# Attention heads with the low parts of the probabilities multiplied last, three outputs in another pool, and the second half of LN1 on ScalarE with a gate behind its transposes

## The chip, the cores and the metric

One Trainium2 chip, one core of it. The metric is the device time in microseconds of one execution; times stand as the median of several runs. A profile is one execution taken by the hardware profiler; its times count from the span's start.

## The reference, cut to what matters

One decoder layer over 512 tokens of width 1024, in float32. All weights are float32 too.

```python
h = layer_norm(x, ln_in_g, ln_in_b)
q_g, k_g, v_g, r_g, a_lr, q_lat, kv_lat, gate_logits = split(h @ w_in)
# branch 1: gated linear attention, 4 heads, chunked        -> y_gla
# branch 2: multi-head latent attention (MLA), 8 heads:
q = (rms_norm(q_lat) @ w_q_b)            # per head 128 "nope" + 64 "rope" columns
kv = (rms_norm(kv_lat[..., :256]) @ w_kv_b)   # per head 128 of k_nope + 128 of v
k_rope = apply_rope(kv_lat[..., 256:])   # shared by the heads
for blk in range(4):                     # 128 queries each, keys [0, block end)
    s = (q_nope @ k_nope.T + q_rope @ k_rope.T) * 192 ** -0.5
    p = softmax(where(causal, s, -inf))
    o[blk] = p @ v
y_mla = merge_heads(o) @ w_o_mla
mix = (g_gla * y_gla + g_mla * y_mla) @ w_out
h = layer_norm(2 ** 0.25 * h + mix, ln1_g, ln1_b)              # LN1
ff = square(relu(h @ w_ff1)) @ w_ff2                            # hidden width 4096
out = layer_norm(2 ** 0.25 * h + ff, ln2_g, ln2_b)
```

## The kernel before, in words

**Numbers in two parts.** A float32 operand is held as a high part (rounded to the matmul's float32r format) and a low part, the remainder. `split` (L111 and L112, with a scale L114 and L115) makes them: ACT writes the high part from PSUM, DVE then subtracts it from the source and writes the low part. A product takes three matmuls, high x high, high x low and low x high; low x low is left out. Weights stream from memory as `wraw` (or `wq`), and `pump` splits them into `whi` and `wlo` in the same way (L189 on ACT, L190 on DVE).

**Who fixes the order.** The program is traced once. Generators ("active") advance by one step at each `tick`, which the gemm helpers call between their steps; so parts of a head, of LN1 or of window sums are traced between matmuls. The tile framework then plans: it runs through the traced instructions with its own model of their times (`schedule_with_timeline_sim=True`), earlier traced ones first where several are ready, gives each tile a slot of its pool, and so fixes one order for each engine. On the chip each engine follows its list in order and waits by semaphores. `tc.issue_after(x)` binds an instruction to come after x on that engine's list.

**PSUM pools.** Eight banks: `pm` has four ("mm" tiles, `MM()`), `px` four ("px" tiles, `PX()`). The gemms of the projections, the feed-forward and the second column of the output take mm tiles; scores, transposes and head outputs take px tiles.

**The MLA heads.** `mla_pair(pr)` projects the queries (`gemm_fm`, 18 matmuls of 512 columns, two accumulators in mm) and keys (12) of heads 2pr and 2pr + 1, starts their generators `mla_head`, and projects their values (`gemm_tm`, 24 matmuls of 256 columns, two mm banks for four tiles; split into `mv` tiles). `mla_head` has four blocks of 128 queries: scores in a px bank (L1051 to L1053 for block 0, L1057 to L1061 for the others: three products of the nope parts, `qn` and `kn`, then two of the rope parts, `QS` and `KK`), mask and maximum on DVE (L1063), exponential with its sum on ACT (L1064), the normalisation on DVE (L1065, L1066). The probabilities are transposed on TensorE (L1078) into three px banks, and split into PT0 (keys 0 to 127), PT1 (128 to 255, and 384 to 511) and PT2 (256 to 383). The output is 12 matmuls in one px bank, for each key tile j: v high x p high (L1097), v high x p low (L1098), v low x p high (L1099). It is split into `omT`. While one head's softmax runs, TensorE works on the projections of the next pair, on the next head's scores or on the projection of the finished heads.

**LN1.** `out` is computed in two halves of 256 tokens, and its `ev_res` (L1407) adds it to the residual rows `res`. `ln1(hf)` normalises tiles 2hf and 2hf + 1: statistics on DVE (L429 to L431), the power -0.5 on POOL (L432), and one pass over the row on DVE (L438). `ln_transpose` then turns the rows on TensorE, two transposes of 128x128 for each of eight k (L447), and makes `h` with gain and bias (L450 on ACT for the high part, L452 on ACT or L454 on DVE, and L455 on DVE for the low part). While `ln1(1)` is under way, the first four blocks of the feed-forward's first weight are multiplied for tokens 0 to 255: `gemm_fm(PL["f1", 0, 0], ..., toks=slice(0, 256))`, 96 matmuls of 256 columns (32 turns of three). For k = 0 to 5 the four accumulators take turns; the last 24 matmuls, k = 6 and 7, follow for one accumulator after another. `finish(t_ln)` stands behind it, then come tokens 256 to 511.

**The window sums.** `win_sums` (L1486) adds and subtracts blocks of the second feed-forward weight on DVE, 128x1024 each, ahead of `win_f2`. They are held behind `st["ev"]` where that exists; before the change it is set by `win_f2` alone, so in the first window nothing holds them.

The lines that `ln_rows` already has for ScalarE, used before the change by the first tile of the input norm alone:

```python
        if on_act:
            nmr = S([P, 1], F32, "nmr")
            stt(nmr, mv[:, 0:1], -1.0, mv[:, 1:2], op0=ALU.mult, op1=ALU.mult)
            act(dst, src, AF.Identity, scale=mv[:, 1:2], bias=nmr)
```

Of the kernel before, what the change touches and what calls it, by code (L numbers as in the profile page):

```python
# [16 lines left out]
ALU = mybir.AluOpType  # L17
AX = mybir.AxisListType

P = 128  # L20
T = 512
D = 1024
NT = T // P
# [29 lines left out]
def tile_hybrid_block(ctx: ExitStack, tc: tile.TileContext, I, out, dbg=None):  # L53
# [178 lines left out]
    def part(x, i, c):  # L232
        return x[i][:, c] if isinstance(x, tuple) else x[:, i, c]

    def gemm_fm(pl, xs, n, evac, width=None, toks=slice(0, T), accs=None, guard=None, late=False):
        na = n // P
        accs = accs or [MM() for _ in range(na)]
        nk = pl["nk"]
        tail = range(nk - 2, nk) if pl["per"] == 2 and nk % 2 == 0 and not late else range(nk - 1, nk)
        turns = [(k, a) for k in range(tail[0]) for a in range(na)] + [(k, a) for a in range(na) for k in tail]  # L240
        for n_, (k, a) in enumerate(turns):
            hi, lo = weights(pl, k)
            xh, xl = part(xs[k], 0, toks), part(xs[k], 1, toks)
            c = slice(a * P, (a + 1) * P)
            o = accs[a][:, toks]
            mm(o, hi[:, c], xh, start=k == 0, stop=False)  # L246
            mm(o, hi[:, c], xl, start=False, stop=False)  # L247
            mm(o, lo[:, c], xh, start=False, stop=k == nk - 1)  # L248
            if (n_ + 1) % na == 0 and n_ + 1 < len(turns):
                tick(width)  # L250
        if guard:
            guard()
        if evac is not None:
            for a in range(na):
                evac(a, accs[a])
                if a == na // 2 - 1:
                    pump(pl["idx"][-1] + 1)
        tick(width)
        return accs
# [166 lines left out]
    def ln_rows(src, dst, mv, on_act=False):  # L426
        bst = S([P, 2, 6], F32, "bst")
        for j in range(2):
            nc.vector.bn_stats(bst[:, j, :], src[:, j * T:(j + 1) * T])  # L429
        nc.vector.bn_aggr(mv, bst)  # L430
        vts(mv[:, 1:2], mv[:, 1:2], LN_EPS, None, op0=ALU.add)  # L431
        gtt(mv[:, 1:2], mv[:, 1:2], mhalf[:, 0:1], op=ALU.pow)  # L432
        if on_act:
            nmr = S([P, 1], F32, "nmr")
            stt(nmr, mv[:, 0:1], -1.0, mv[:, 1:2], op0=ALU.mult, op1=ALU.mult)
            act(dst, src, AF.Identity, scale=mv[:, 1:2], bias=nmr)
        else:
            vts(dst, src, mv[:, 0:1], mv[:, 1:2], op0=ALU.subtract, op1=ALU.mult)  # L438

    def ln_transpose(rows, g, b, outs, hf, alt=False, n="h0"):  # L440
        tk = slice(hf * 256, (hf + 1) * 256)
        for k in range(NK):
            if len(outs) <= k:
                outs.append(A([P, 2, T], F32R, n) if n == "h0" else (B([P, T], F32R, n), B([P, T], F32R, n)))
            p = MM() if alt and k in (4, 5) else PX()
            for i in range(2):
                nc.tensor.transpose(p[:, i * P:(i + 1) * P], rows[2 * hf + i][:, k * P:(k + 1) * P], ident)  # L447
            tmp = B([P, 256], F32, "lnt")
            hi, lo = part(outs[k], 0, tk), part(outs[k], 1, tk)
            ha = act(hi, p[:, :256], AF.Identity, scale=g[:, k:k + 1], bias=b[:, k:k + 1])  # L450
# [583 lines left out]
    def mla_head(h, hl, qn, kn, vt):  # L1034
# [5 lines left out]
        for i in range(NT):  # L1040
            n = P * (i + 1)
            c = slice(i * P, (i + 1) * P)
            p = PX()
            o = p[:, :n]
            Pm = P02[:, :P] if i == 0 else P02[:, P:] if i == 2 else B([P, T], F32, "Pm")
            Pm = Pm[:, :n]
            mx = S([P, 1], F32, "mx")
            sme = S([P, 1], F32, "sme")
            if i == 0:
                o2 = p[:, :2 * P].rearrange("p (w n) -> p w n", w=2)  # L1050
                mm(o2, qn[:, 0, c], kn[:, :, :n], start=True, stop=False, skip_group_check=True)  # L1051
                mm(o, qn[:, 1, c], kn[:, 0, :n], start=False, stop=False, skip_group_check=True)
                mm(o2, qs[:, c], KK[:, :, :n], start=False, stop=True, skip_group_check=True)  # L1053
                vtt(Pm, p[:, P:2 * P], hide[:, T - n:], op=ALU.add)
                first = Pm
            else:
                mm(o, qn[:, 0, c], kn[:, 0, :n], start=True, stop=False)  # L1057
                mm(o, qn[:, 0, c], kn[:, 1, :n], start=False, stop=False)
                mm(o, qn[:, 1, c], kn[:, 0, :n], start=False, stop=False)
                mm(o, qs[:, c], KK[:, 0, :n], start=False, stop=False)  # L1060
                mm(o, qs[:, c], KK[:, 1, :n], start=False, stop=True)  # L1061
                first = hide[:, T - n:]
            nc.vector.tensor_tensor_reduce(Pm, o, first, -1.0, 3e38, op0=ALU.add, op1=ALU.min, accum_out=mx)  # L1063
            act(Pm, Pm, AF.Exp, bias=mx, scale=-1.0, accum_out=sme)  # L1064
            nc.vector.reciprocal(sme, sme)  # L1065
            vts(Pm, Pm, sme, None, op0=ALU.mult)  # L1066
            Ps.append(Pm)
            if i != 0:
                yield
# [12 lines left out]
        PT0, PT1, PT2 = PT  # L1082
        while vt[NT - 1] is None:
            yield
        o = PX()
        for j in range(NT):
            c = slice(hl * P, (hl + 1) * P)
            vh, vl = vt[j][:, 0, c], vt[j][:, 1, c]
            if j == 0:
                ph, pl, od = PT0[:, 0, :], PT0[:, 1, :], o  # L1090
            elif j == 1:
                ph, pl, od = PT1[:, 0, :384], PT1[:, 1, :384], o[:, 128:]
            elif j == 2:
                ph, pl, od = PT2[:, 0, :], PT2[:, 1, :], o[:, 256:]
            else:
                ph, pl, od = PT1[:, 0, 384:], PT1[:, 1, 384:], o[:, 384:]
            mm(od, vh, ph, start=j == 0, stop=False)  # L1097
            mm(od, vh, pl, start=False, stop=False)  # L1098
            mm(od, vl, ph, start=False, stop=j == NT - 1)  # L1099
        yield  # L1100
        om = A([P, 2, T], F32R, "omT")
        st["om"] = split(o, om[:, 0, :], om[:, 1, :])
# [316 lines left out]
    def ln1(hf):  # L1419
        for tt in (2 * hf, 2 * hf + 1):  # L1420
            mv = S([P, 2], F32, "mv")
            ln_rows(res[tt], res[tt], mv)
        yield
        for k, _ in enumerate(ln_transpose(res, ln1g, ln1b, h1T, hf, n="h1")):
            if k % 2:
                yield
# [5 lines left out]
    finish(t_ln)  # L1432
    st["gates"] = st["ln"]
    t_ln = spawn(ln1(1))
    accs = gemm_fm(PL["f1", 0, 0], h1T, T, None, toks=slice(0, 256))
    finish(t_ln)

    def residual1():
# [283 lines left out]
```

## Time and profile before

| | |
|---|---|
| median of 3 runs | 871.4 us (871.12 to 872.61) |
| profiled execution | 870.4 us, its span 868.6 us |
| TensorE busy | 849.6 us, 98% of the span, 4709 matmuls |
| VectorE busy | 635.7 us, 73% |
| ScalarE busy | 470.8 us, 54% |
| GpSimd busy | 146.2 us, 17% |
| mean granted TensorE clock | 0.997 |

In the profile's rows, a line of the timeline has the start, the duration, the engine, the kernel's line, the operation, the tile written and the tiles read, partitions x elements, and how many were merged; in brackets the idle time of that engine before it and what ended it. Matmuls overlap: the next starts before the one before has ended, so the pace is read from start to start. Rows of "waits" give the waiter, the releaser, the total in us, how often, and the longest. Rows by stretch give the length, then busy time and number of instructions for PE, PEld, DVE, ACT and POOL, the granted TensorE clock, and the DMA engines' share and rate.

### The profile page before, as it was taken

The page shows a single profiled execution, that of the slowest core. Times are in us where ns is not written, and L with a number is a line of the kernel's source. Part 1 is how long each engine was busy: PE and PEld are TensorE (multiplying, and loading weights), DVE is VectorE, ACT ScalarE, POOL GpSimd, SP SyncE. Part 2 cuts the span into 40 slices and gives each one's busy share as a digit, 9 for nine tenths or more (in the row PEclk, how much of TensorE's full clock was granted, in tenths as well). Part 3 has the DMA queues.
Part 4 walks back from the last instruction along what each step waited for, and adds up shares of the span by engine and source line. Part 5 has one row for each costly group of instructions (what it writes and reads, how often), then busy time and mean ns, then how long its engine had stood idle before and what let it go on. Part 6 is the DMA issues. An engine that isn't in the chain of part 4 may idle for free.

```text
span 868.6 us, 12771 instructions
## 1 busy us (share of the span) xinstructions
PE 849.6 (98%) x4709; PEld 743.7 (86%) x4709; DVE 635.7 (73%) x1084; ACT 470.8 (54%) x828; POOL 146.2 (17%) x186
## 2 busy tenths in 40 slices
PE   5999999999999999999999999999999999999996
PEld 5988888889999988888888888988888888889985
DVE  7859989969566548567666888986567546888875
ACT  6546777656475625355554323485366446766820
POOL 0223304221110030300000022005301520141000
PEclk9999999999999999999999999999999999999998
DMA  7994946696647434322136346008922990499311
GB/s 246 288 231 145 325 161 169 167 318 195 146 146 165 140 100 125 79 68 91 49 133 229 124 140 224 1 1 257 258 67 49 295 217 21 101 243 236 115 58 73
DMA packets 95214, 134.58 MB, mean 155 GB/s; under 512 B 12672, under 2 KB 58112, under 8 KB 95152
## 3 DMA queue, kind: packets, MB, share of 16 engines
q1 hardware_dynamic: 73840, 92.36, 33.3%
q0 software_dynamic: 19392, 37.76, 20.3%
q10 hardware_dynamic: 1920, 3.66, 1.1%
q8 instruction: 37, 0.61, 0.3%
q14 instruction: 25, 0.20, 0.1%
HBM read 110.15 MB, written 8.91 MB: 137 GB/s over the span
## 4 chain that ended last, share of the span: by engine, by line
PE 95%; DMA 2%; DVE 2%; ACT 1%; issue 0%; POOL 0%; POOLq 0%; SPq 0%; DVEq 0%; ACTq 0%
PE mm L246 11%; PE mm L247 11%; PE mm L248 11%; PE mm L282 5%; PE mm L283 5%; PE mm L284 5%; PE mm L1248 4%; PE mm L1247 4%; PE mm L1246 4%; PE px L1534 3%; PE px L1535 3%; PE px L1533 3%; PE mm L1534 2%; PE mm L1535 2%; PE mm L1533 2%; PE mm L752 1%
## 5 line engine op out<-in xcount | busy, mean ns | idle before, releaser
L190 DVE TENSOR_TENSOR wlo<-wraw,whi 128x1024 fp32r<-128x1024 f32 (+1 forms) x90 | 98.8, 1098 | 80.6 <-ACT whi L189 75.1
L189 ACT ACTIVATE whi<-wraw 128x1024 fp32r<-128x1024 f32 (+1 forms) x90 | 85.4, 949 | 84.0 <-PE mm L247 44.5
L247 PE MATMUL mm<-h,whi 128*128 128x512 f32 x224 | 87.2, 389 | 0.0
L246 PE MATMUL mm<-h,whi 128*128 128x512 f32 x224 | 86.9, 390 | 0.0
L248 PE MATMUL mm<-h,wlo 128*128 128x512 f32 x224 | 83.4, 390 | 0.0
L190 DVE TENSOR_TENSOR wlo<-wq,whi 128x1024 fp32r<-128x1024 f32 x44 | 53.8, 1224 | 28.2 <-ACT whi L189 27.9
L1552 POOL DMA_DIRECT2D res<-ev x42 | 37.5, 1009 | 180.9 <-ACT ev L1550 145.5
L189 ACT ACTIVATE whi<-wq 128x1024 fp32r<-128x1024 f32 x44 | 46.5, 1058 | 27.4 <-PE mm L1247 17.1
L1248 PE MATMUL mm<-sh,wlo 128*128 128x256 f32 x176 | 50.0, 284 | 0.0
L1246 PE MATMUL mm<-sh,whi 128*128 128x256 f32 x176 | 50.0, 284 | 0.0
L1247 PE MATMUL mm<-sh,whi 128*128 128x256 f32 x176 | 49.8, 283 | 0.0
L248 PEld LDWEIGHTS mm<-h,wlo 128*128 128x128 f32 x224 | 42.0, 188 | 9.0 <-DVE wlo L190 0.4
L247 PEld LDWEIGHTS mm<-h,whi 128*128 128x128 f32 x224 | 42.1, 188 | 8.8
L246 PEld LDWEIGHTS mm<-h,whi 128*128 128x128 f32 x224 | 42.1, 188 | 8.7
L189 ACT ACTIVATE xh<-wraw 128x1024 fp32r<-128x1024 f32 (+1 forms) x28 | 27.3, 984 | 29.6 <-PE mm L284 14.9
L190 DVE TENSOR_TENSOR xl<-wraw,xh 128x1024 fp32r<-128x1024 f32 (+1 forms) x28 | 31.2, 1127 | 10.7 <-ACT xh L189 10.7
L1595 ACT ACTIVATE relu<-mm 128x512 f32<-128x512 f32 x24 | 14.2, 594 | 41.2 <-PE mm L248 41.2
L1248 PEld LDWEIGHTS mm<-sh,wlo 128*128 128x128 f32 x176 | 33.8, 192 | 0.0
L1247 PEld LDWEIGHTS mm<-sh,whi 128*128 128x128 f32 x176 | 33.8, 192 | 0.0
L1246 PEld LDWEIGHTS mm<-sh,whi 128*128 128x128 f32 x176 | 33.8, 192 | 0.0
L1246 PE MATMUL mm<-h,whi 128*128 128x256 f32 x112 | 32.0, 286 | 0.0
L1248 PE MATMUL mm<-h,wlo 128*128 128x256 f32 x112 | 31.9, 284 | 0.0
(502 smaller groups left out, 2687.0 us busy)
## 6 DMA issues: line engine op xcount, KB each, us to landing
wraw<-in_w_ff_dram SPq DMA_DIRECT2D x36, 512.0 KB, 5.0
wraw<-in_w_in_dram SPq DMA_DIRECT2D x30, 512.0 KB, 5.1
wq<-in_w_ff_dram POOLq DMA_DIRECT2D x26, 512.0 KB, 9.7
res<-ev POOLq DMA_DIRECT2D x42, 256.0 KB, 9.4
wq<-in_w_in_dram SPq DMA_DIRECT2D x20, 512.0 KB, 7.3
wq<-in_w_in_dram POOLq DMA_DIRECT2D x18, 512.0 KB, 9.6
hsd<-hs SPq DMA_DIRECT2D x16, 256.0 KB, 4.2
xr<-hsd SPq DMA_DIRECT2D x16, 256.0 KB, 5.1
```

Source lines behind the costliest of these rows:

```text
L189: st["ins"] = act(hi[:, :nk, :n], raw[:, :nk, :n], AF.Copy)
L190: st["lo"] = vtt(lo[:, :nk, :n], raw[:, :nk, :n], f(hi[:, :nk, :n]), op=ALU.subtract)
L246: mm(o, hi[:, c], xh, start=k == 0, stop=False)
L247: mm(o, hi[:, c], xl, start=False, stop=False)
L248: mm(o, lo[:, c], xh, start=False, stop=k == nk - 1)
L282: mm(o, xh, hi[:, :n], start=opens, stop=False, skip_group_check=share)
L283: mm(o, xh, lo[:, :n], start=False, stop=False, skip_group_check=share)
L284: mm(o, xl, hi[:, :n], start=False, stop=last, skip_group_check=share)
L1246: mm(oa, hi[:, k, c], xh, start=opens and k == 0 and a == 0, stop=False, skip_group_check=True)
L1247: mm(oa, hi[:, k, c], xl, start=False, stop=False, skip_group_check=True)
L1248: mm(oa, lo[:, k, c], xh, start=False, stop=k == 3, skip_group_check=True)
L1533: mm(o, xh[:, c], hi[:, pp], start=opens, stop=False, skip_group_check=True)
```

## The change

- In `mla_head` the scores begin with the rope products (`QS` x `KK`) and end with the nope products, in all blocks.
- The output's 12 matmuls are ordered anew: for the four key tiles first v high x p high and v low x p high, and then the four products with the probabilities' low parts.
- The outputs of heads 2, 3 and 4 take an mm tile instead of a px tile.
- `ln1(1)` passes `on_act=True`: the pass over rows 2 and 3 goes from DVE (L438) to ACT (L436), with one 128x1 operation on DVE (L435) for each. That operation is stored in `st["ev"]`, so the first window's sums are now held behind it on DVE.
- `ln1(1)` waits three ticks longer before it traces its transposes. The half gemm over tokens 0 to 255 gets `behind="tp"`: its last 24 matmuls are placed behind the last transpose that has been traced when they begin, which is that of k = 3; so the transposes of four k stand ahead of them on TensorE.

```diff
-    def gemm_fm(pl, xs, n, evac, width=None, toks=slice(0, T), accs=None, guard=None, late=False):
+    def gemm_fm(pl, xs, n, evac, width=None, toks=slice(0, T), accs=None, guard=None, late=False, behind=None):
...
-            mm(o, hi[:, c], xh, start=k == 0, stop=False)
-            mm(o, hi[:, c], xl, start=False, stop=False)
-            mm(o, lo[:, c], xh, start=False, stop=k == nk - 1)
+            with ExitStack() as gates:
+                if behind and k in tail:
+                    gates.enter_context(tc.issue_after(tp.ins if (k, a) != (tail[0], 0) else (tp := st[behind]).ins))
+                mm(o, hi[:, c], xh, start=k == 0, stop=False)
+                mm(o, hi[:, c], xl, start=False, stop=False)
+                mm(o, lo[:, c], xh, start=False, stop=k == nk - 1)
...
-            stt(nmr, mv[:, 0:1], -1.0, mv[:, 1:2], op0=ALU.mult, op1=ALU.mult)
+            st["ev"] = stt(nmr, mv[:, 0:1], -1.0, mv[:, 1:2], op0=ALU.mult, op1=ALU.mult)
...
-                nc.tensor.transpose(p[:, i * P:(i + 1) * P], rows[2 * hf + i][:, k * P:(k + 1) * P], ident)
+                st["tp"] = nc.tensor.transpose(p[:, i * P:(i + 1) * P], rows[2 * hf + i][:, k * P:(k + 1) * P], ident)
...
-                mm(o2, qn[:, 0, c], kn[:, :, :n], start=True, stop=False, skip_group_check=True)
-                mm(o, qn[:, 1, c], kn[:, 0, :n], start=False, stop=False, skip_group_check=True)
-                mm(o2, qs[:, c], KK[:, :, :n], start=False, stop=True, skip_group_check=True)
+                mm(o2, qs[:, c], KK[:, :, :n], start=True, stop=False, skip_group_check=True)
+                mm(o2, qn[:, 0, c], kn[:, :, :n], start=False, stop=False, skip_group_check=True)
+                mm(o, qn[:, 1, c], kn[:, 0, :n], start=False, stop=True, skip_group_check=True)
...
-                mm(o, qn[:, 0, c], kn[:, 0, :n], start=True, stop=False)
+                mm(o, qs[:, c], KK[:, 0, :n], start=True, stop=False)
+                mm(o, qs[:, c], KK[:, 1, :n], start=False, stop=False)
+                mm(o, qn[:, 0, c], kn[:, 0, :n], start=False, stop=False)
                 mm(o, qn[:, 0, c], kn[:, 1, :n], start=False, stop=False)
-                mm(o, qn[:, 1, c], kn[:, 0, :n], start=False, stop=False)
-                mm(o, qs[:, c], KK[:, 0, :n], start=False, stop=False)
-                mm(o, qs[:, c], KK[:, 1, :n], start=False, stop=True)
+                mm(o, qn[:, 1, c], kn[:, 0, :n], start=False, stop=True)
...
-        o = PX()
-        for j in range(NT):
-            c = slice(hl * P, (hl + 1) * P)
+        o = MM() if 2 <= h < 5 else PX()
+        c = slice(hl * P, (hl + 1) * P)
+        late = []
+        for j, pt, w in ((0, PT0, slice(0, T)), (1, PT1, slice(0, 384)), (2, PT2, slice(0, 256)), (3, PT1, slice(384, T))):
             vh, vl = vt[j][:, 0, c], vt[j][:, 1, c]
...
+            ph, pl, od = pt[:, 0, w], pt[:, 1, w], o[:, j * P:]
             mm(od, vh, ph, start=j == 0, stop=False)
-            mm(od, vh, pl, start=False, stop=False)
-            mm(od, vl, ph, start=False, stop=j == NT - 1)
+            mm(od, vl, ph, start=False, stop=False)
+            late.append((od, vh, pl))
+        for j, ops in enumerate(late):
+            mm(*ops, start=False, stop=j == NT - 1)
...
-            ln_rows(res[tt], res[tt], mv)
-        yield
+            ln_rows(res[tt], res[tt], mv, on_act=hf == 1)
+        for _ in range(1 + 3 * hf):
+            yield
...
-    accs = gemm_fm(PL["f1", 0, 0], h1T, T, None, toks=slice(0, 256))
+    accs = gemm_fm(PL["f1", 0, 0], h1T, T, None, toks=slice(0, 256), behind="tp")
```

More of the change, by code (lines that the diff above doesn't have):

```diff
@@ L1084, in mla_head @@
             yield
-        o = PX()
-        for j in range(NT):
-            c = slice(hl * P, (hl + 1) * P)
+        o = MM() if 2 <= h < 5 else PX()
+        c = slice(hl * P, (hl + 1) * P)
+        late = []
+        for j, pt, w in ((0, PT0, slice(0, T)), (1, PT1, slice(0, 384)), (2, PT2, slice(0, 256)), (3, PT1, slice(384, T))):
             vh, vl = vt[j][:, 0, c], vt[j][:, 1, c]
[L1089 to L1096, printed above, removed]
+            ph, pl, od = pt[:, 0, w], pt[:, 1, w], o[:, j * P:]
             mm(od, vh, ph, start=j == 0, stop=False)
-            mm(od, vh, pl, start=False, stop=False)
-            mm(od, vl, ph, start=False, stop=j == NT - 1)
+            mm(od, vl, ph, start=False, stop=False)
+            late.append((od, vh, pl))
+        for j, ops in enumerate(late):
+            mm(*ops, start=False, stop=j == NT - 1)
         yield
```

## The prediction, made before the change was run

> **What bounds the kernel now.** Read first: the page's totals and its chain of work; then TensorE's waits; then two stretches of the span; then the timeline, engine by engine, around each wait.
>
> ```profile
> span 868.6 us, 12771 instructions
> PE 849.6 (98%) x4709; PEld 743.7 (86%) x4709; DVE 635.7 (73%) x1084; ACT 470.8 (54%) x828; POOL 146.2 (17%) x186
> PE 95%; DMA 2%; DVE 2%; ACT 1%; issue 0%; POOL 0%; POOLq 0%; SPq 0%; DVEq 0%; ACTq 0%
> ...
> PE px L1057 <- DVE PT L112: 1.2, 1, 1.2
> PE px L1098 <- DVE PT L112: 1.1, 1, 1.1
> ...
> 404.00:424.00 20.00, 17.36 (x106) 15.18 (x105) 16.65 (x48) 12.57 (x32) 0.00 (x0) 1.00 0.32 106
> 553.00:573.00 20.00, 20.00 (x95) 16.78 (x94) 20.00 (x28) 14.13 (x23) 0.00 (x0) 1.00 0.00 1
> ```
>
> TensorE carries 95% of the chain and no matmul is removed, so only its gaps can be won, and the list of its waits names two in touched code, both in the attention heads: L1057, a head's second block of scores, waits for VectorE's split of the transposed probabilities (PT); L1098, a head's output, waits for the low part of PT. The third place is the half gemm behind LN1, whose rows follow. In the stretch 404 to 424, after the three engines' busy times, the clock column is 1.00: these gaps cost only their own length.
>
> What a gap costs is read from start to start, since matmuls overlap:
>
> ```profile
> 404.46 0.33 PE L1053 MATMUL px<-KK,QS 128*128 128x256 f32 x1
> 405.98 0.36 PE L1057 MATMUL px<-qn,qn 128*128 128x256 f32 x1 [1.19 <-DVE PT L112]
> ...
> 418.89 0.60 PE L1078 MATMUL px<-ca,Pm 128*128 128x128 f32 x4
> 419.86 0.50 PE L1097 MATMUL px<-PT,mv 128*128 128x512 f32 x1 [0.37 <-ACT PT L111]
> 421.45 0.50 PE L1098 MATMUL px<-PT,mv 128*128 128x512 f32 x1 [1.09 <-DVE PT L112]
> ...
> 422.18 0.39 PE L1057 MATMUL px<-qn,qn 128*128 128x512 f32 x1
> 422.41 0.39 PE L1058 MATMUL px<-qn,qn 128*128 128x512 f32 x1
> ...
> 423.81 0.27 PE L1078 MATMUL px<-ca,P 128*128 128x128 f32 x1
> 423.92 0.27 PE L1078 MATMUL px<-ca,Pm 128*128 128x128 f32 x1
> ...
> 539.66 0.28 PE L246 MATMUL mm<-h,xh 128*128 128x256 f32 x1
> 539.78 0.28 PE L247 MATMUL mm<-h,xh 128*128 128x256 f32 x1
> 540.02 1.03 PE L447 MATMUL px<-ca,res 128*128 128x128 f32 x8
> 541.38 0.74 PE L246 MATMUL mm<-h,xh 128*128 128x256 f32 x4 [0.33 <-ACT h L450]
> 541.96 0.43 PE L447 MATMUL px<-ca,res 128*128 128x128 f32 x2
> 542.42 0.39 PE L247 MATMUL mm<-h,xh 128*128 128x256 f32 x1
> ```
>
> Unhindered steps: 0.23 for 512 columns (422.18 to 422.41), 0.12 for 256 (539.66 to 539.78), 0.11 for a transpose (423.81 to 423.92). Then: place 1, 405.98 - 404.46 - 0.12 = 1.40 lost. Place 2, 419.86 - 418.89 - 4 x 0.11 = 0.53, and 421.45 - 419.86 - 0.23 = 1.36, together 1.89. Place 3 (LN1), 541.38 - 540.02 - 8 x 0.11 = 0.48, and 542.42 - 541.96 - 2 x 0.11 = 0.24, together 0.72. All three: 4.01 us.
>
> **The change, part by part.**
>
> *Scores with the rope part first.* The same five matmuls (three in block 0) in another order: no cost, and no gain that a row shows, as place 1 waits for a bank, not for operands.
>
> *Low parts last, place 2.* What the output needs, and when:
>
> ```profile
> 419.23 1.07 ACT L111 ACTIVATE PT<-px 128x512 fp32r<-128x512 f32 x2
> 420.66 0.40 ACT L111 ACTIVATE PT<-px 128x256 fp32r<-128x256 f32 x1
> ...
> 419.57 1.22 DVE L190 TENSOR_TENSOR wlo<-wraw,whi 128x1024 fp32r<-128x1024 f32 x1
> 420.71 1.28 DVE L112 TENSOR_TENSOR PT<-px,PT 128x512 fp32r<-128x512 f32 x2
> ...
> 404.12 1.34 ACT L111 ACTIVATE PT<-px 128x512 fp32r<-128x512 f32 x3
> 405.15 0.69 DVE L112 TENSOR_TENSOR PT<-px,PT 128x512 fp32r<-128x512 f32 x1
> ```
>
> High parts come from ACT, low parts from DVE, which at 419.57 first splits a weight for 1.22. Today L1098 multiplies the low part as second of twelve. With the eight high matmuls first: both 512-column ones from 419.86 end their steps at 420.32; the 384-column pair needs PT1's high part (419.23 + 1.07 = 420.30) and goes to 420.67 at three quarters of 0.23 each; the 256 pair waits for 420.66 + 0.40 = 421.06, a gap of 0.4. By then PT0's low part (420.71 + 0.64 = 421.35) is nearly there, and the next head's 512-column scores, 5 x 0.23 = 1.15, stand between as they do now. So 1.36 becomes about 0.4: gain 1.0, between 0 (no bank, below) and 1.89.
>
> *Three outputs in the other pool, place 1.* At 404.46 head 4's scores need a px bank; the four are held by head 3's three PT blocks and by block 0 of the scores, and the first comes free at 405.15 + 0.69 = 405.84. Head 3's output could not start for the same reason. With its output in an mm bank and its high parts first, it can go ahead of the scores as soon as ACT has PT0 (about 404.12 + 0.54 = 404.66, half of the 1.07 that two such splits took at 419.23). It then has 2 x 0.23 + 2 x 0.17 + 2 x 0.12 + 2 x 0.11 = 1.26 of work, until 405.98, where the scores start today. 1.40 becomes 0.2: gain 1.2, between 0 (order kept) and 1.40. A loss is possible too, for mm banks are scarce:
>
> ```profile
> 402.49 0.63 ACT L189 ACTIVATE whi<-wraw 128x512 fp32r<-128x512 f32 x1 [2.67 <-PE mm L247]
> ...
> 406.88 0.68 DVE L115 SCALAR_TENSOR_TENSOR qn<-mm,qn 128x512 fp32r<-128x512 f32 x1
> 412.14 0.42 DVE L112 TENSOR_TENSOR mv<-mm,mv 128x256 fp32r<-128x256 f32 x1
> 421.91 0.68 DVE L112 TENSOR_TENSOR qn<-mm,qn 128x512 fp32r<-128x512 f32 x1
> ...
> 433.17 0.36 ACT L111 ACTIVATE mv<-mm 128x256 fp32r<-128x256 f32 x1
> ```
>
> At place 1 two mm banks hold values that are read until 412.14 + 0.42, two hold the queries of the next pair, the first of them until 406.88 + 0.68 = 407.56. At place 2 it is 421.91 + 0.68 = 422.59, and the values' banks are read only from 433.17. So the gain needs an accumulator split earlier. ACT stood idle for 2.67 before 402.49, so there is room, and the planner draws the order anew; I take the gain at both places, not as certain.
>
> *LN1 of tiles 2 and 3.*
>
> ```profile
> 532.74 0.15 DVE L431 TENSOR_SCALAR mv<-mv 128x1 f32<-128x1 f32 x1
> 534.08 1.23 DVE L1486 TENSOR_TENSOR wq<-wq,wq 128x1024 f32<-128x1024 f32 x1
> 535.22 1.53 DVE L438 TENSOR_SCALAR res<-res,mv 128x1024 f32<-128x1024 f32 x2
> ...
> 532.97 1.48 POOL L432 TENSOR_TENSOR mv<-mv,mhalf 128x1 f32<-128x1 f32 x1 [0.46 <-DVE mv L431]
> ...
> 540.76 1.93 ACT L450 ACTIVATE h<-px,cb 128x256 fp32r<-128x256 f32 x4 [9.73 <-PE px L447]
> ...
> L438 DVE TENSOR_SCALAR res<-res,mv x4: 807/810/814, 510.5 to 535.9; 128x1024 f32<-128x1024 f32 x4
> L436 ACT ACTIVATE x<-x,nmr,mvin x1: 1240/1240/1240, 7.4 to 7.4; 128x1024 f32<-128x1024 f32 x1
> ```
>
> Removed from DVE: two passes (1.53 together). Added: two one-column operations, 0.15 each by L431, and two ACT passes of 1.24 by the L436 row. Tile 3's power ends at 532.97 + 1.48 = 534.45; nmr at 534.60; the row at 535.84, instead of 536.75, where the pass stood behind a window sum (534.08, 1.23). The sums (L1486) now wait on DVE for tile 3's nmr; they start about 1.8 later than now (the first followed L431 at 532.74), but the two passes are gone, and three sums of 1.23 from 534.6 end at 538.3, before the transposes of today. That counts, since DVE is busy 20.00 of 20 from 553 to 573.
>
> The gate is a new wait on TensorE: eight transposes stand ahead of the last 24 matmuls of the half gemm, and these and all behind them wait if the rows are late. The 24 begin 24 x 0.12 = 2.88 before 540.02, at 537.14: 1.3 after the row. Eight transposes take 0.88; the 24 matmuls then cover the splits for which TensorE waits today (1.36 from the first transpose to L246); the remaining eight transposes find h of k = 0 ready behind them. The 0.72 goes; I take 0.6, as two more changes between transposes and matmuls cost about 0.05 to 0.1 each (541.96 to 542.42 holds one). Bounds: 0.72 gained, and a loss where the rows come after 537.14. No DMA is moved, and nothing is moved past another step on SP's or POOL's queue; the power on POOL stays where it is.
>
> A rule speaks against this part: the Trainium skill, "ScalarE: Activation LUTs", section "Rules for kernel authors", says to give additions and multiplications to VectorE, not ScalarE. The rows agree on the price (1.24 against 0.81). By the rule the rows would be later than now (the second rival, 869.1); by the rows of DVE's queue they are earlier, as DVE is the late one here, and the sum keeps that.
>
> **Sum.** 1.0 + 1.2 + 0.6 = 2.8. The profiled execution took 870.4 (span 868.6 and 1.8 around it): 867.6. The median of the runs shown, 871.4, is 1.0 above it: 868.6.
>
> **Rivals.**
> - *The heads' waits only change their name*: an output waits for an mm bank (407.56, 422.59) instead of PT. For it: the four rows above. Then LN1 alone pays: 871.4 - 0.6 = 870.8. With one place of the two: 871.4 - 0.6 - 1.1 = 869.7.
> - *ScalarE is late*: other work stands ahead of its passes, and they only take the place of DVE's, each 1.24 - 0.81 = 0.43 longer. Then the rows come at 536.75 + 0.86 = 537.61, 0.47 after TensorE asks for them; LN1 gives 0.6 - 0.47 = 0.13: 869.1. Against it: ACT idles for 9.73 before 540.76 today.
> - *Slower: the projections lack a bank.* The 18 query matmuls of the next pair (18 x 0.23 = 4.1) fill TensorE until head 3's transposes. If an output holds a bank while both accumulators are due, half of them (2.1) finds no place; at two heads 4.2, less LN1's 0.6: 875.0. It decides where nothing else is ready in the 2.1; against it, one accumulator can run through all three k alone.
>
> **How the numbers follow.** Forecast (both head places and LN1) 0.45; ScalarE late 0.08; one head place 0.14, halved between faster and same as 869.7 lies on the bound; LN1 alone 0.21; too few banks 0.12. A measurement tells about 0.2% (1.7 us) from no change. So faster 0.60, same 0.28, slower 0.12. Low end: all 4.01 won, 867.4, and 0.3 for the runs' spread below their median: 867.1. High end: LN1 alone, 870.8, with the 1.2 of the spread above: 872.0. The forecast's own range is 867.4 to 869.6.
>
> **What would show it.** Right: no L1057 or output wait for PT of over 0.5 between 400 and 425; all output low parts in a row; L447's first eight near 537, the next TensorE wait for h gone, ACT L436 twice near 533 to 536. Wrong: new waits of mm matmuls or of the output for "qn" or "mv" splits, or TensorE idle ahead of L447. What would make it wrong as a whole is a redrawn order with gaps elsewhere in 330 to 460, where the list of waits has none but these.

## The result, and the profile after

| kernel | median, us | its runs | ratio to before |
|---|---|---|---|
| before | 871.4 | 870.99 to 873.18 | |
| after | 867.61 | 866.97 to 869.95 | 0.9957 [0.9938, 0.9976] |

The change makes the kernel 3.8 us faster by the medians. The forecast was 2.8 faster, 868.6 us in a range of 867.1 to 872.0. One execution of all that are reported here, of e8 below, was a slow one (1218.77 us at a granted clock of 0.657, where the others have 0.997 to 0.999); e8's median, 870.29, is 870.16 without it.

The first lines of after's page (span; busy time of each engine; shares of the chain of work that ended last) and the longest of TensorE's waits (waiter, releaser, total, how often, the longest):

```profile
span 868.2 us, 12767 instructions
PE 849.6 (98%) x4709; PEld 743.9 (86%) x4709; DVE 635.0 (73%) x1084; ACT 472.7 (54%) x830; POOL 144.7 (17%) x186
PE 94%; DMA 2%; DVE 1%; ACT 1%; issue 0%; POOL 0%; POOLq 0%; SPq 0%; DVEq 0%; ACTq 0%
...
PE px L450 <- DMA wraw<-in_w_in_dram: 10.1, 1, 10.1
...
PE mm L1094 <- ACT PT L111: 0.4, 1, 0.4
```

Lines of after stand 3 below those of before: L249 to L251 are the gemm's L246 to L248, L450 the transposes' L447, L1081 the probabilities' L1078. The lines of the new code do not follow that: of the scores L1054, L1060 and L1061 are the rope products, and of the output L1094 is v high x p high, L1095 v low x p high and L1098 v high x p low. The two waits for DVE's PT (1.2 and 1.1) are gone; the longest that is left in the heads is one of 0.4, for ACT's PT. The other rows here lie in parts that the change does not touch; that of 10.1 is the start of the program, and the last section says what it waits for. But the two profiled spans differ by 0.4 only, 868.6 against 868.2, where the medians differ by 3.8. (The profiled execution of after took 869.95, the longest of its five.) So the span has to be cut where the programs part. On TensorE both run the same matmuls in the same order up to a product late in the query gemm of heads 0 and 1. Mark A is this last shared one, mark B the first matmul of the half gemm behind LN1's first half. Before, then after:

```profile
326.43 0.39 PE L247 MATMUL mm<-latT,whi 128*128 128x512 f32 x1
...
528.50 0.28 PE L246 MATMUL mm<-h,xh 128*128 128x256 f32 x1
```

```profile
329.44 0.39 PE L250 MATMUL mm<-latT,whi 128*128 128x512 f32 x1
...
528.84 0.28 PE L249 MATMUL mm<-h,xh 128*128 128x256 f32 x1
```

Up to A, where nothing was changed, this execution of after is 3.01 later. From A to B (the heads) it takes 199.40 instead of 202.07, 2.67 less; from B to the end (LN1's second half and all behind it) 868.2 - 528.84 = 339.4 instead of 340.1, 0.7 to 0.8 less. Together 3.46 less. That is the change's own gain; what stands before A differs without a difference in the code, as the table of the experiments shows.

Where the heads' 2.67 come from, on the timeline of TensorE and, behind it, of ACT and DVE, after, place 1:

```profile
402.83 0.28 PE L1054 MATMUL px<-KK,QS 128*128 128x256 f32 x1
...
403.30 0.66 PE L1081 MATMUL px<-ca,Pm 128*128 128x128 f32 x4
404.32 0.50 PE L1094 MATMUL mm<-PT,mv 128*128 128x512 f32 x1 [0.36 <-ACT PT L111]
404.65 0.39 PE L1095 MATMUL mm<-PT,mv 128*128 128x512 f32 x1
404.88 0.39 PE L249 MATMUL mm<-latT,whi 128*128 128x512 f32 x1
...
406.72 0.39 PE L251 MATMUL mm<-latT,wlo 128*128 128x512 f32 x1
406.95 0.33 PE L1094 MATMUL mm<-PT,mv 128*128 128x384 f32 x1
...
403.67 1.36 ACT L111 ACTIVATE PT<-px 128x512 fp32r<-128x512 f32 x3 [0.18 <-PE px L1081]
...
404.30 0.69 DVE L112 TENSOR_TENSOR PT<-px,PT 128x512 fp32r<-128x512 f32 x1
```

Block 0 of the next head's scores (402.83) now stands ahead of head 3's transposes, and nothing between these and its output. The output starts 404.32 - 403.30 - 4 x 0.11 = 0.58 after its transposes have left TensorE: it now asks for PT0's high part as soon as ACT can have it. Two output matmuls, then nine query matmuls of the next pair (404.88 to 406.72), then the rest of the output: no step waits for a px bank any more. Of the 1.40 of this place 0.58 is left, 0.82 is gained.

Place 2, after, the same engines:

```profile
416.09 0.60 PE L1081 MATMUL px<-ca,Pm 128*128 128x128 f32 x4
...
417.23 0.34 PE L1064 MATMUL px<-qn,qn 128*128 128x384 f32 x1
417.41 0.40 PE L1094 MATMUL mm<-PT,mv 128*128 128x512 f32 x1
417.64 0.40 PE L1095 MATMUL mm<-PT,mv 128*128 128x512 f32 x1
...
421.90 0.62 PE L1098 MATMUL mm<-PT,mv 128*128 128x512 f32 x2
...
417.27 0.69 DVE L112 TENSOR_TENSOR PT<-px,PT 128x512 fp32r<-128x512 f32 x1
```

Head 4's output follows scores of the next head without a gap (417.23 to 417.41, the pace of 384 columns), and the low-part products (L1098) come 4.5 after the first of the output, when PT0's low part has been there since 417.27 + 0.69 = 417.96. All 1.89 of this place are gained.

LN1, after, ACT's two passes, POOL's power for the second of the rows, and TensorE:

```profile
532.72 2.38 ACT L439 ACTIVATE res<-res,nmr,mv 128x1024 f32<-128x1024 f32 x2 [1.96 <-DVE nmr L438]
...
532.70 0.55 POOL L435 TENSOR_TENSOR mv<-mv,mhalf 128x1 f32<-128x1 f32 x1 [0.46 <-DVE nmr L438]
...
537.47 1.04 PE L450 MATMUL px<-ca,res 128*128 128x128 f32 x8
538.26 0.36 PE L249 MATMUL mm<-h,xh 128*128 128x256 f32 x1
538.47 0.28 PE L250 MATMUL mm<-h,xh 128*128 128x256 f32 x1
```

The rows are ready at 532.72 + 2.38 = 535.10. The first eight transposes start when 72 matmuls have run from B (528.84 + 72 x 0.12 = 537.48), and 0.79 later the last 24 matmuls follow, with no wait. The 0.72 of this place are gone.

### The profile page after: what moved, and what is told of

It is laid out like the page before. It is cut to its first block, busy times and chain, and to the rows that moved or that the text cites. A ratio compares the mean times of both kernels' runs of the same rounds, so it can differ in the third digit from the quotient of the medians.

```text
span 868.2 us, 12767 instructions
## 1 busy us (share of the span) xinstructions
PE 849.6 (98%) x4709; PEld 743.9 (86%) x4709; DVE 635.0 (73%) x1084; ACT 472.7 (54%) x830; POOL 144.7 (17%) x186
## 4 chain that ended last, share of the span: by engine, by line
PE 94%; DMA 2%; DVE 1%; ACT 1%; issue 0%; POOL 0%; POOLq 0%; SPq 0%; DVEq 0%; ACTq 0%
PE mm L249 11%; PE mm L250 11%; PE mm L251 11%; PE mm L287 5%; PE mm L285 5%; PE mm L286 5%; PE mm L1247 4%; PE mm L1246 4%; PE mm L1245 4%; PE px L1535 3%; PE px L1533 3%; PE px L1534 3%; PE mm L1535 2%; PE mm L1533 2%; PE mm L1534 2%; DMA wraw<-in_w_in_dram 2%
## 5 line engine op out<-in xcount | busy, mean ns | idle before, releaser
L249 PE MATMUL mm<-h,whi 128*128 128x512 f32 x224 | 86.9, 390 | 0.0
L251 PE MATMUL mm<-h,wlo 128*128 128x512 f32 x224 | 83.4, 390 | 0.0
L251 PEld LDWEIGHTS mm<-h,wlo 128*128 128x128 f32 x224 | 42.0, 188 | 9.1 <-DVE wlo L190 0.4
L249 PEld LDWEIGHTS mm<-h,whi 128*128 128x128 f32 x224 | 42.1, 188 | 8.6
```

## The experiments

Each kernel's one profiled execution is cut at A and B. "Before" in a row is the median of before's runs beside it.

| kernel | median | before | ratio, 95% | start to A | A to B | B to end |
|---|---|---|---|---|---|---|
| before | 871.4 | | | 326.43 | 202.07 | 340.12 |
| after | 867.61 | 871.4 | 0.9957 [0.9938, 0.9976] | 329.44 | 199.40 | 339.33 |
| after_again | 867.50 | 871.05 | 0.9965 [0.9953, 0.9976] | 328.11 | 199.41 | 339.24 |
| e1_ln1_only | 869.90 | 870.74 | 0.9987 [0.9979, 0.9996] | 327.74 | 202.10 | 339.19 |
| e2_heads_only | 869.28 | 870.74 | 0.9980 [0.9971, 0.9989] | 327.73 | 199.38 | 340.39 |
| e3_all_in_px | 869.78 | 870.74 | 0.9988 [0.9979, 0.9997] | 327.27 | 202.39 | 339.43 |
| e4_old_scores | 866.60 | 870.74 | 0.9947 [0.9934, 0.9959] | 326.50 | 199.01 | 339.18 |
| e4_again | 866.89 | 871.05 | 0.9953 [0.9940, 0.9965] | 328.62 | 199.01 | 339.23 |
| e5_low_last_only | 869.42 | 871.61 | 0.9978 [0.9969, 0.9987] | 326.20 | 200.73 | 340.50 |
| e6_banks_only | 868.38 | 871.61 | 0.9968 [0.9955, 0.9981] | 326.39 | 199.19 | 340.92 |
| e7_act_only | 871.47 | 871.61 | 1.0002 [0.9992, 1.0011] | 326.17 | 202.05 | 340.10 |
| e8_gate_only | 870.29 | 871.61 | 0.9988 [0.9978, 0.9998] | 327.24 | 202.11 | 339.30 |
| e9_heads_3_4 | 866.95 | 871.05 | 0.9948 [0.9936, 0.9960] | 325.88 | 198.67 | 339.18 |
| e10_heads_0_to_4 | 869.99 | 871.05 | 0.9983 [0.9974, 0.9991] | 328.64 | 200.73 | 339.17 |

How to read it: A to B is the same within 0.06 wherever the heads' code is the same (202.05 to 202.11 in before, e1, e7, e8; 199.38 to 199.41 in after, after_again, e2; 199.01 twice). Start to A is the same code in all of them and takes 325.88 to 329.44. The medians carry that scatter; the two stretches behind A do not. So a median can say something else than the stretches: e2 is 1.46 below before by the medians and 2.42 from A to the end, e6 3.23 by the medians and 2.08 from A to the end. The readings below go by the stretches, each from one execution; after and e4, with two executions each, agree within 0.1 in both.

**The theory**: three separate gains, two from the heads (a px bank is missing, and the low parts are late), one from LN1. **Its rivals**: the bank and the order only work together; the ScalarE pass, not the order on TensorE, pays in LN1; or the difference of the medians is chance.

**e1_ln1_only: after, with the scores and the output of before.**

```diff
-        o = MM() if 2 <= h < 5 else PX()
+        o = PX()
...
-            mm(od, vl, ph, start=False, stop=False)
-            late.append((od, vh, pl))
-        for j, ops in enumerate(late):
-            mm(*ops, start=False, stop=j == NT - 1)
+            mm(od, vh, pl, start=False, stop=False)
+            mm(od, vl, ph, start=False, stop=j == NT - 1)
```

(and the scores' five matmuls in the order of before)

> Only the LN1 part of the change: rows 2 and 3 on ScalarE, transposes of four k ahead of the last 24 matmuls, window sums held; the heads as before. Theory (three separate places, each worth what TensorE lost there): the loss behind the half gemm, 0.72 us, goes to under 0.15; the two gaps of the heads stay at 1.40 and 1.89 us; 0.6 to 0.9 us faster than before (about 870.6). Rival (the LN1 part only moves a wait, and the whole gain is that of the heads): a new wait of 0.5 us or more ahead of the transposes, no change in time.

B to end is 0.93 shorter, A to B as before. TensorE's two waits of before are back, in its list of waits:

```profile
PE px L1060 <- DVE PT L112: 1.2, 1, 1.2
PE px L1101 <- DVE PT L112: 1.1, 1, 1.1
```

**e2_heads_only: before, with the scores and the output of after.**

```diff
-        o = PX()
+        o = MM() if 2 <= h < 5 else PX()
...
+            mm(od, vl, ph, start=False, stop=False)
+            late.append((od, vh, pl))
+        for j, ops in enumerate(late):
+            mm(*ops, start=False, stop=j == NT - 1)
```

> Only the heads' part: rope scores first, low parts last, three outputs in mm banks; LN1 as before. Theory: the loss of 0.72 us behind the half gemm stays, the two gaps of the heads fall from 3.3 us together to about 0.6 as in the changed kernel: 2.5 to 3 us faster than before (about 868.6). Rival (the parts need each other, since the order is drawn anew for the whole): under 1.5 us or over 3.5 us.

A to B is 2.69 shorter, as in after. B to end is 0.27 longer than before's. From A to the end e1 gains 0.90 and e2 2.42, together 3.32, where after gains 3.46: the parts add up, and the heads carry the larger. By its median, 1.46 faster, e2 would have met the rival of its expectation; the stretch does not bear that out.

**e3_all_in_px: after, with every output in a px bank.**

```diff
-        o = MM() if 2 <= h < 5 else PX()
+        o = PX()
```

> The changed kernel with all outputs in px banks. Theory (place 1 was a wait for a px bank, so it is the other pool that lets head 3's output go ahead): the gap near 404 comes back, 1.0 to 1.4 us, and place 2 stays closed: 0.8 to 1.4 us slower than the changed kernel, still 2 us or more faster than before. Rival (low parts last does it all, the pool is indifferent): no gap over 0.6 us at 404, the time of the changed kernel.

A to B takes 202.39, 0.32 longer than before: the whole gain of the heads is gone, and the expectation of a gain of over 2 us was wrong. TensorE's timeline in e3, at place 1 and at a new place:

```profile
405.46 0.22 PE L1056 MATMUL px<-qn,qn 128*128 128x128 f32 x1
406.99 0.36 PE L1060 MATMUL px<-KK,QS 128*128 128x256 f32 x1 [1.30 <-DVE PT L112]
...
431.10 0.22 PE L1056 MATMUL px<-qn,qn 128*128 128x128 f32 x1
432.40 0.36 PE L1060 MATMUL px<-KK,QS 128*128 128x256 f32 x1 [1.07 <-DVE PT L112]
```

L1060 reads KK and QS, not PT: what it waits for is the px bank that DVE's split of PT sets free. Place 1 is back as it was, and the last pair's heads have the same wait now. At place 2 this kernel loses 0.54 and 0.31, read as in e5 below, so the order of the low parts gains 1.04 of the 1.89 there; but place 1 and the new wait take it all back, and without the mm bank low parts last and rope first together bring nothing.

**e4_old_scores and, repeated, e4_again: after, with the scores' order of before.**

```diff
-                mm(o, qs[:, c], KK[:, 0, :n], start=True, stop=False)
-                mm(o, qs[:, c], KK[:, 1, :n], start=False, stop=False)
-                mm(o, qn[:, 0, c], kn[:, 0, :n], start=False, stop=False)
+                mm(o, qn[:, 0, c], kn[:, 0, :n], start=True, stop=False)
                 mm(o, qn[:, 0, c], kn[:, 1, :n], start=False, stop=False)
-                mm(o, qn[:, 1, c], kn[:, 0, :n], start=False, stop=True)
+                mm(o, qn[:, 1, c], kn[:, 0, :n], start=False, stop=False)
+                mm(o, qs[:, c], KK[:, 0, :n], start=False, stop=False)
+                mm(o, qs[:, c], KK[:, 1, :n], start=False, stop=True)
```

(block 0 likewise)

> The changed kernel with the scores in their old order, nope products first. Theory (the prediction's: the order of the scores is worth nothing): the losses of the changed kernel, its time within 0.5 us. Rival (rope products that are ready early fill TensorE while keys are still being split, and this draws the order anew): gaps of 0.5 us or more come back in 330 to 425, 1 us or more slower than the changed kernel.

> The changed kernel with the scores in their old order, once more, on the chip of the changed kernel. Theory (rope products first cost a little, by more changes between unlike matmuls and a redrawn order behind): 538.2 from the shared matmul to the end, 0.5 us less than the changed kernel, its median 0.3 to 1.0 us lower. Rival (the first reading was chance): within 0.2 us of it from the shared matmul.

A to B is 199.01 both times, against 199.40 and 199.41 with the rope part first: the new order of the scores costs 0.39. No single wait carries it. In e4 as in after one step of TensorE in the heads is over 0.2 late, by 0.52 in both (the step from place 1's last transpose to the output); the 0.39 is spread over many small steps, and why they differ stays open. Neither the expectation nor its rival had a gain. The medians point the same way (866.89 against 867.50 beside each other), but their intervals overlap.

**after_again: after, unchanged.**

> The changed kernel once more, beside the next one. Theory (up to the first matmul whose order differs the program is the same in all kernels, and the 326.4 to 329.4 us to there are chance of the execution): the stretch from the shared matmul to the end again 538.7, within 0.3 us, whatever the time to there. Rival (the change makes the early part slower, as 329.4 against 326.4 of before suggests): over 328.5 to there again.

867.50, and 199.41 and 339.24 behind A: the gain stands, and the 869.95 of after's profiled execution was its first part.

**e5_low_last_only: before, with the low parts last, all outputs in px, scores as before.**

```diff
-            mm(od, vh, pl, start=False, stop=False)
-            mm(od, vl, ph, start=False, stop=j == NT - 1)
+            mm(od, vl, ph, start=False, stop=False)
+            late.append((od, vh, pl))
+        for j, ops in enumerate(late):
+            mm(*ops, start=False, stop=j == NT - 1)
```

> The kernel before with the low parts last alone; scores, banks and LN1 as before. Theory (the order of the products helps only where the output has a bank): place 1 stays at 1.4 us, place 2 falls from 1.89 to under 1.0; from the last instruction that all orders share to the end, up to 1 us less than the 542.2 us of before, unless a new gap of about 1 us opens near 430 as with all outputs in px banks. Rival (the low parts last are the gain): 2 us or more less.

A to B is 1.34 shorter, half of the heads' gain. TensorE in e5: the wait for a px bank has moved to the last pair,

```profile
428.30 0.33 PE L1053 MATMUL px<-KK,QS 128*128 128x256 f32 x1
429.70 0.36 PE L1057 MATMUL px<-qn,qn 128*128 128x256 f32 x1 [1.07 <-DVE PT L112]
```

429.70 - 428.30 - 0.12 = 1.28 lost, nearly the 1.40 of place 1, which is gone here; the expectation had it stay. At place 2:

```profile
416.98 0.60 PE L1078 MATMUL px<-ca,Pm 128*128 128x128 f32 x4
417.94 0.50 PE L1091 MATMUL px<-PT,mv 128*128 128x512 f32 x1 [0.36 <-ACT PT L111]
...
418.71 0.34 PE L1092 MATMUL px<-PT,mv 128*128 128x384 f32 x1
419.19 0.38 PE L1091 MATMUL px<-PT,mv 128*128 128x256 f32 x1
```

417.94 - 416.98 - 4 x 0.11 = 0.52 and 419.19 - 418.71 - 0.17 = 0.31 are left of 1.89, so the order alone gains 1.06 there. Against e3, which has the rope products first and the outputs in px as well, e5's A to B is 1.66 shorter (200.73 against 202.39): the order of the scores costs more where a px bank is short.

**e6_banks_only: before, with nothing but the pool of three outputs.**

```diff
-        o = PX()
+        o = MM() if 2 <= h < 5 else PX()
```

> The kernel before with heads 2, 3 and 4 writing their outputs to mm banks, high and low parts in the old order. Theory (both are needed): place 1 loses less than 1.4 us only as far as the second product of the output has its low part; 0.5 to 1.5 us of the 3.3 remain, 1 to 2 us less from the shared point to the end. Rival (the bank alone is the gain): 2.4 us or more less, as with the whole heads' part. Second rival (the projections lack a bank): new waits of mm matmuls, slower than before.

A to B is 2.88 shorter, more than with the whole change of the heads (2.67). One line does it: with the three outputs out of px, TensorE has the bank for the next scores, and the order that the planner then draws puts other work between PT's split and the product with its low part (L1098). TensorE in e6, at the outputs of heads 3 and 4:

```profile
400.96 0.50 PE L1097 MATMUL mm<-PT,mv 128*128 128x512 f32 x1 [0.36 <-ACT PT L111]
...
403.97 0.40 PE L1098 MATMUL mm<-PT,mv 128*128 128x512 f32 x1
...
414.12 0.39 PE L1097 MATMUL mm<-PT,mv 128*128 128x512 f32 x1
...
417.16 0.40 PE L1098 MATMUL mm<-PT,mv 128*128 128x512 f32 x1
```

The low part is asked for 3.0 after the high part, both times without a wait. That the order low parts last is needed too has fallen; beside the banks it is worth 199.19 - 199.01 = 0.18. B to end is 0.80 longer than before's, so from A to the end e6 gains 2.08. The 0.80 comes from one wait far behind:

```profile
PE px L1248 <- DVE wlo L190: 0.5, 1, 0.5
```

It is near 780, not in the code of the change: TensorE waits for a weight's low part. DVE has the order of before there but waits for ACT's high part of an earlier weight, and ACT has idled 4.24 for the transfer of `ev` to `res`, where it idles 2.36 in before. Why that transfer lands later is open; the kernels without LN1's part are 0.27 to 0.80 longer than before's there (e2, e5, e6), those with it agree within 0.26.

**e7_act_only and e8_gate_only: LN1's part in two.** e7 is before with the ScalarE pass alone (window sums not held, no gate, the transposes not delayed); e8 is before with the gate and the three ticks, the pass left on DVE.

```diff
 e7:
-            ln_rows(res[tt], res[tt], mv)
+            ln_rows(res[tt], res[tt], mv, on_act=hf == 1)
 e8:
-        yield
+        for _ in range(1 + 3 * hf):
+            yield
...
-    accs = gemm_fm(PL["f1", 0, 0], h1T, T, None, toks=slice(0, 256))
+    accs = gemm_fm(PL["f1", 0, 0], h1T, T, None, toks=slice(0, 256), behind="tp")
```

> The kernel before with the passes over rows 2 and 3 on ScalarE, and nothing else: no gate, no later transposes, window sums not held. Theory (it is the gate that counts, since the rows were ready at 536.75 and TensorE came to the transposes at 540.02): the loss of 0.72 us stays at 0.5 or more, no change in time. Rival (earlier rows let the planner put the transposes forward by itself): loss under 0.2.

> The kernel before with the gate and the later transposes, the passes staying on VectorE and the window sums not held. Theory: the rows come near 536.75 and the gate asks for them near 537.1, so the loss is under 0.3 us, 0.6 to 0.9 less from the shared point to the end, as with the whole LN1 part. Rival (the gate needs ScalarE's earlier rows): TensorE idles 0.5 us or more ahead of the first transposes, no gain or a loss.

e7 changes nothing (B to end 340.10, before 340.12); e8 gains 0.82 there, where e1, with the whole of LN1's part, gains 0.93. In e7 the rows are ready at 534.51 + 2.38 = 536.89 and the transposes stand where they stood, behind all the matmuls:

```profile
534.51 2.38 ACT L436 ACTIVATE res<-res,nmr,mv 128x1024 f32<-128x1024 f32 x2 [4.38 <-DVE nmr L435]
...
539.73 1.04 PE L447 MATMUL px<-ca,res 128*128 128x128 f32 x8
541.09 0.75 PE L246 MATMUL mm<-h,xh 128*128 128x256 f32 x4 [0.33 <-ACT h L450]
```

In e8, with the rows from DVE, the transposes come forward and no wait follows:

```profile
535.46 1.53 DVE L441 TENSOR_SCALAR res<-res,mv 128x1024 f32<-128x1024 f32 x2
...
537.99 1.04 PE L450 MATMUL px<-ca,res 128*128 128x128 f32 x8
538.78 0.36 PE L249 MATMUL mm<-h,xh 128*128 128x256 f32 x1
```

The rows end at 536.99 and are asked for at 537.99: DVE was early enough for the gate by 1.0. The gate pays; the ScalarE pass and the held sums have nothing to win beyond the 0.11 between e1 (339.19) and e8 (339.30), and two executions of after differ by 0.09 (339.33, 339.24).

Counted from B, the rows end 8.25 later in before (536.75 - 528.50) and 7.64 in e8, both on DVE; 8.67 in e7, on ScalarE (B at 326.17 + 202.05 = 528.22); and 6.26 in after (535.10 - 528.84). So the engine alone brings the rows no earlier: in e7 ScalarE's pass waits for `nmr`, which stands behind two window sums on DVE. Only the kernels that hold the sums have early rows. No run holds the sums and leaves the pass on DVE, so what ScalarE adds to the hold is not shown.

**e9_heads_3_4 and e10_heads_0_to_4: e4 with other heads in mm.**

```diff
 e9:
-        o = MM() if 2 <= h < 5 else PX()
+        o = MM() if 3 <= h < 5 else PX()
 e10:
-        o = MM() if 2 <= h < 5 else PX()
+        o = MM() if h < 5 else PX()
```

> As the one before (old score order), but only heads 3 and 4 write to mm banks, head 2 to a px bank. Theory (the two places belong to head 3's and head 4's outputs): the same 0.5 to 0.7 us of gaps between 390 and 425, 538.2 to 538.7 from the shared matmul to the end. Rival (head 2's px bank is what lets the rest go ahead): a gap of 1 us or more comes back.

> As the second one (old score order), but heads 0 to 4 write to mm banks, five instead of three. Theory (mm banks are not scarce while the planner can run one accumulator alone): no new gap over 0.5 us, 538.2 to 539 from the shared matmul to the end. Rival (the prediction's slower case, projections lack a bank): matmuls of the gemms wait for omT or mv splits, 1 to 4 us more.

e9 has 198.67, the shortest A to B of all. Its list of TensorE's waits names no output and no scores; besides the start it has one row:

```profile
PE px L450 <- ACT x L439: 8.7, 1, 8.7
PE mm L249 <- DVE rt L1002: 0.2, 1, 0.2
```

The two outputs on which the prediction argued (heads 3 and 4) suffice, and without head 2's the wait that after and e4 still have at place 1 is gone too. e9 beats before (0.9948) and stands ahead of after by 0.73 and 0.15 in the two stretches; by the medians, 866.95 against 867.50, the two are not told apart. With five outputs in mm (e10) A to B is 200.73, by a new wait in e10:

```profile
370.26 0.80 PE L1098 MATMUL mm<-PT,mv 128*128 128x512 f32 x4
...
372.24 0.50 PE L1094 MATMUL mm<-PT,mv 128*128 128x512 f32 x1 [1.18 <-ACT PT L111]
```

The expectation, no new gap over 0.5, missed this. The row names PT, which L1094 reads, and no mm bank: these probabilities had left TensorE by 358.3, and ACT makes their high part only at 371.59, behind the split of the output before (`omT`, 371.10), after idling 1.65. TensorE has no other work placed between the two outputs.

## Why the prediction was right, point by point

- **What bounds the kernel, and the three places**: right. The page's TensorE time did not change (849.6 both times), and the gain is 0.82 + 1.89 + 0.72 = 3.43 of the 4.01 lost there, where the two stretches give 3.46.
- **Place 1** (term 1.2): the mechanism, a missing px bank, was right; the term was too large. It was to leave 0.2 and left 0.58, as the planner put block 0 of the next scores ahead of the transposes: the step had left it between the transposes and the output, where it covers ACT's split of PT0.
- **Place 2** (term 1.0): too small by 0.89. The prediction gave the gain to the order of the low parts and kept 0.53 and 0.4 of waiting for ACT. That is what the order does by itself, 1.06 in e5 and 1.04 in e3. But with the output in another pool it no longer follows directly on its transposes: scores stand between, and the 0.53 and the 0.4 go too. e6 shows that the pool brings this by itself, so the ascription, *low parts last* for place 2 and *three outputs in the other pool* for place 1, was the step that failed: the banks alone bring both (e6, 2.88), the order alone 1.34 (e5), and beside the banks the order adds 0.18.
- **Scores with the rope part first** (term 0): 0.39 of cost, by e4. The argument, the same five matmuls, overlooked that the planner draws TensorE's order in the heads anew from it.
- **LN1** (term 0.6): 0.72 of gaps, 0.79 and 0.88 by the stretch. The 0.05 to 0.1 that each change between transposes and matmuls was to cost did not appear: from the first transpose to the second matmul behind the eight it is 538.47 - 537.47 = 1.00, which is 8 x 0.11 + 0.12. Counted from B, the gate asked when it was to ask (537.47 - 528.84 = 8.63; worked out 537.14 - 528.50 = 8.64), and the rows came at 6.26 instead of 7.34. POOL's power for tile 3 ended at 4.41 instead of 5.95, by 0.61 since it started earlier and by 0.93 since it took 0.55 instead of 1.48: in before a window sum runs on DVE beside it, and in after the sums are held. Which half of the part pays was not said in the prediction: it is the gate (e8), not the engine (e7).
- **The rule against ScalarE** (the Trainium skill, "ScalarE: Activation LUTs", section "Rules for kernel authors"): with the pass alone on ScalarE (e7) the rows came later than on DVE, as by the rule (8.67 behind B against 8.25), though there too the wait is for DVE, whose two window sums stand ahead of `nmr`. The prediction's answer, that they come earlier since DVE's queue is the late one, holds only with the window sums held (6.26). TensorE did not need them earlier in any of these kernels, so here neither the rule nor breaking it is worth a measurable time.
- **The rivals.** *The waits only change their name*: no mm matmul waits for a qn or mv split in after; the one new wait is 0.4 for PT. *ScalarE is late*: it idles 1.96 ahead of its two passes, and TensorE asks 2.37 after they end. *The projections lack a bank*: the nine query matmuls of one accumulator run in one piece behind the first two of the output (404.88 to 406.95), as the counter-argument had it, and five outputs in mm (e10) cost no such wait either.
- **The sum**: 2.8 forecast, 3.46 measured behind A, 3.8 by the medians of the first comparison and 3.55 by those of the second. Place 2 and LN1 gave 1.0 more than their terms, place 1 0.4 less, and the heads' stretch as a whole 2.67 where 2.2 was summed. The sum came near partly by luck: the misses of the two head places, 0.4 and 0.9, go opposite ways. That the median lies 0.3 further out is within what the stretch before A varies.

## What to carry to other kernels

A wait that the profile puts down to the reader of a tile can be a wait for that tile's bank: look whether the waiting instruction reads the tile at all, and if not, try to give the bank to another pool before changing any order. Change one edit at a time where a planner draws the order anew, since an edit that removes nothing and adds nothing (the scores' order) cost 0.39, and one line (the pool) was worth more in the heads, 2.88, than all their edits together, 2.67. And measure from the last instruction that two programs share: behind it two executions agreed within 0.1 us, while whole executions of one kernel differ by up to 3.65 (866.79 to 870.44 in after_again).

## What the runs showed of the hardware

**The same program, 325.88 to 329.44 us.** The matmuls up to A are the same, in the same order, in all fourteen profiled executions, and their time varies by 3.56. After's 3.01 more than before, followed matmul by matmul, arise mainly at two places. By the first matmul after is 1.42 late (10.10 against 8.68, the wait at the start), by the 300th 1.61 (65.17 against 63.56); the 850th is still 1.61 late (174.75 against 173.14), the 950th 2.97 (194.30 against 191.33), and from the 1000th (203.17 against 200.16) to A it stays at 3.01. At the start it is a block of the input x that lands later, on which DVE's statistics wait; at the second place it is a weight, on which ACT's split waits. Before, then after:

```profile
6.60 0.69 DVE L429 BATCH_NORM_STATS2 bst<-x 128x6 f32<-128x512 f32 x1 [0.26 <-DMA x<-in_x_dram]
...
183.69 1.06 ACT L189 ACTIVATE whi<-wraw 128x1024 fp32r<-128x1024 f32 x1 [2.96 <-DMA wraw<-in_w_in_dram]
```

```profile
8.02 0.69 DVE L432 BATCH_NORM_STATS2 bst<-x 128x6 f32<-128x512 f32 x1 [1.85 <-DMA x<-in_x_dram]
...
186.66 1.06 ACT L189 ACTIVATE whi<-wraw 128x1024 fp32r<-128x1024 f32 x1 [4.33 <-DMA wraw<-in_w_in_dram]
```

8.02 - 6.60 is the 1.42 of the start, and 186.66 - 183.69 the 2.97 behind the second place. The list of waits puts the start of after down to a weight's transfer (10.1), but the transposes that wait there read x and no weight. The granted clock is 1.00 in both executions from 0 to 20 and from 180 to 200, so it is not the clock. What makes the transfers land later in one execution than in another stays open.

**A GpSimd operation beside a VectorE one.** The power for tile 3 in `ln1(1)`, 128x1 on POOL, took 1.48 in all six profiled executions in which a window sum (128x1024, two inputs) ran on DVE beside it (before, e2, e5, e6, e7, e8), and 0.55 in all eight in which the sums were held until later.
